# A hybrid decoder layer: the last gate chunk adds its earlier sums on VectorE instead of preloading them into PSUM, and two gate steps are held back around the last transposes

## The chip, the cores and the metric

The kernel runs on one core of one Trainium2 chip. The metric is the time of one execution on the device in microseconds (us), as the median of several runs. Besides, one execution was profiled: its trace gives the start and length of each engine's instructions, and its span, from the first to the last of them, is a little shorter than its time.

TensorE (PE in the profile; its weight loads are PEld) multiplies, VectorE (DVE) and ScalarE (ACT) work on elements, GpSimd (POOL) does too but cannot read PSUM, and SyncE (SP) issues the loads and the stores.

## The reference, cut to what matters

The layer has 256 tokens and a width of 2048, all in float32. The change lies in its last two formulas:

```
h    = h + HierMoE(RMSNorm(h))                 # 32 experts, each token goes to two
gate = sigmoid(RMSNorm(h, norm_ple) @ W_g)     # W_g: 2048 x 2048 (w_ple_gate)
out  = h + gate * (p @ W_p)                    # p @ W_p is ready long before
```

Each expert ends in a product with its `w_down` (512 x 2048). The sum over the experts is `h`, and the gate multiplies `h`, scaled by `norm_ple`, with `W_g`. The factor of the RMSNorm that belongs to a token is applied at the end, as the scale of the sigmoid, so that the product can begin before all of `h` is there.

## The kernel before

The kernel is written for one instruction order, engine by engine: what stands first in the code is issued first on its engine, and nothing reorders it. All weights flow through one ring of 26 buffers of 1 MB. `want` lists the loads in the order in which SP issues them, `pump` issues as many as have a buffer, and `free` gives buffers back.

The columns of `h` are made in four chunks of 512 (`TC`, numbers 0 to 3). Experts are handled in eight waves of four (`w` = 0 to 7). At the end of the program the columns of chunks 2 and 3 still miss the waves 4 to 7. `down_wave(w, ...)` (L1103) is the product of one wave with 512 columns of `w_down`: 32 matmuls at L1109 that need four loads of 1 MB. `outputs` (L1062) evicts it as a high part `yh` (ScalarE, L1065) and a low part `yl` (VectorE, L1066), and `scatter` (L1069) adds both to the sum over waves, `po`. After wave 7, `add_down` (L1115) adds `po` to `h` (called `acc`, in the trace `x`), `rows(ci)` (L1136) transposes the chunk on TensorE (L1145), scales it (VectorE, L1148) and splits it into a high part (ScalarE, L1151) and a low part (VectorE, L1152), both in `hs`. `squares` (L1154) sums the squares for the RMSNorm.

The gate's product for a chunk `ci` is cut into eight steps (`pg_steps`): the step `k = 2n + q` multiplies 256 of the chunk's 512 rows of `W_g` (the half `q`) with the block `n` of 512 output columns. `gate_step` (L1160) is 12 matmuls of 128 x 512 (L1170 to L1172) over two token halves `tt`: high times high, high times low, low times high. `prep_pg` (L1125) prepares the weights of a step with `split` (L344): ScalarE casts the high part (L346), and then VectorE subtracts to get the low part (L347), into one of three buffers `wsq`. It is called one and two steps ahead. Two steps complete a block: for chunks 0 to 2 VectorE then adds it to the sum so far, `gs` (L1196; `macc` in the trace).

These 24 steps of the chunks 0 to 2 stand in the list `todo`, and `steps(n)` takes the next `n` of them. They are strewn between the down waves as work for TensorE while loads and evictions go on. `W_g` arrives in loads of 1 MB, two for each half of a chunk's 2048 output columns; `halves_` says behind which down wave's loads each pair stands.

The last chunk comes when `todo` is empty. Its result must be the sum over all four chunks. `preload(n)` brings `gs` into the PSUM block by a product with the identity in float32 (L1275, two matmuls, four records in the trace), and the chunk's own steps add to it there. A finished block goes through the sigmoid (ScalarE, L1300, straight from PSUM), is multiplied by `ple` and added to `acc` (VectorE, L1301 and L1302), and is stored (SP, L1303).

Of the kernel before, what the change touches and what calls it, by code (L numbers as in the profile page):

```python
# [11 lines left out]
AF = mybir.ActivationFunctionType  # L12
# [18 lines left out]
def kernel(ctx: ExitStack, tc: tile.TileContext, I, out):  # L31
    nc = tc.nc
# [28 lines left out]
    loads, nxt, arrived = [], [0], {}  # L61
# [18 lines left out]
    def free(n=1):  # L80
        used[0] -= n
        pump()

    def ps():
        return PS.tile([128, 512], F32, name="pst", tag="ps")

    def pa():
        return PA.tile([128, 2, 512], F32, name="pat", tag="pa")

    def w2(shape, name, dt=F32):  # L90
        return W.tile(shape, dt, name=name, tag="w2", bufs=4)
# [79 lines left out]
                want(("ple", k), [128, 2048], w_ple[128 * k:128 * k + 128, :])  # L171

    order = [(2, w) for w in range(NROW, NW)] + [(3, w) for w in range(NROW, NW)]
    halves_ = [(0, 1), (1, 0), (1, 1), (2, 0), None, (2, 1), None, (3, 0)]
    for (ci, w), nxt_ in zip(order, halves_):
        want_d(w, *TC[ci])
        if nxt_:
# [39 lines left out]
    ident = C.tile([128, 128], F32, name="ident")  # L217
# [125 lines left out]
    def split(i, src, shape, eng=nc.vector, copy=nc.scalar.copy):  # L343
        wsl.append(wsl.pop(0))  # L344
        t = wsl[-1].rearrange("p (a s b) -> p a s b", a=shape[0], s=2)
        copy(t[:, :, 0], src)  # L346
        eng.tensor_sub(t[:, :, 1], src, t[:, :, 0].bitcast(F32))  # L347
        wsp[i] = t
# [448 lines left out]
    for i, (kind, a, b, q) in enumerate(granules):  # L797
        if i < n_in:
            group, start, stop = a, b == 0 and q == 0, b == 1 and q == 1
        else:  # L800
            group, start, stop = "o", (i - n_in) % 4 == 0, (i - n_in) % 4 == 3
# [5 lines left out]
        pt = pts[group]  # L807
# [292 lines left out]
    rs5 = C.tile([128, 2, 1], F32, name="rs5")  # L1100
    last = len(TC) - 1
# [13 lines left out]
    def add_down(po, c0, cn):  # L1115
        for tt in range(2):
            nc.vector.tensor_add(acc[tt][:, c0:c0 + cn], po[:, tt], acc[tt][:, c0:c0 + cn])

    def pg_steps(ci):
        return [(n, q) for n in range(4) for q in range(TC[ci][1] // 256)]  # L1120
# [4 lines left out]
    def prep_pg(ci, i):  # L1125

        upto = granules.index((ci, 0)) + i
        while done[0] <= min(upto, len(granules) - 1):
            c, k = granules[done[0]]
            done[0] += 1  # L1130
            n, q = pg_steps(c)[k]
            split((c, k), arrived["pg", c, n // 2, q][:, :, 512 * (n % 2):512 * (n % 2) + 512], [2, 512])
            if n % 2:
                free()

    def rows(ci):  # L1136

        c0, cn = TC[ci]
        kn, k0 = cn // 128, c0 // 128
        hs = hsb[ci % 2]  # L1140
        src = []
        for tt in range(2):
            src.append(ps().rearrange("p (k t) -> p k t", k=4))
            for kk in range(kn):
                nc.tensor.transpose(src[tt][:, kk], acc[tt][:, c0 + 128 * kk:c0 + 128 * kk + 128], ident)  # L1145
        for tt in range(2):
            tm = w2([128, 4, 128], "tm")
            nc.vector.tensor_tensor(tm, src[tt],  # L1148
                                    g_ple[:, k0:k0 + kn, None].to_broadcast([128, kn, 128]), op=OP.mult)
            hh = hs[:, :, 128 * tt:128 * tt + 128]  # L1150
            nc.scalar.copy(hh, tm)  # L1151
            nc.vector.tensor_sub(hs[:, :, 256 + 128 * tt:384 + 128 * tt], tm, hh.bitcast(F32))  # L1152

    def squares(ci):  # L1154
        c0, cn = TC[ci]
        for tt in range(2):
            scr = w2([128, 512], "scr")
            nc.scalar.activation(scr, acc[tt][:, c0:c0 + cn], AF.Square, accum_out=ss5[:, tt, ci:ci + 1])

    def gate_step(ci, i, pt, start):  # L1160
        n, q = pg_steps(ci)[i]
        kn = TC[ci][1] // 128
        hs = hsb[ci % 2]
        ws = wsp.pop((ci, i))
        for tt in range(2):
            for kk in range(2):
                b = 2 * q + kk
                mh = hs[:, b, 128 * tt:128 * tt + 128]
                ml = hs[:, b, 256 + 128 * tt:384 + 128 * tt]
                nc.tensor.matmul(pt[tt], mh, ws[:, kk, 0], start=start and b == 0, stop=False)  # L1170
                nc.tensor.matmul(pt[tt], mh, ws[:, kk, 1], start=False, stop=False)  # L1171
                nc.tensor.matmul(pt[tt], ml, ws[:, kk, 0], start=False, stop=b == kn - 1)  # L1172

    def two(kind):
        if kind:
            return [ps(), ps()]
        pt = pa()
        return [pt[:, 0], pt[:, 1]]

    def gate_product(ci):  # L1180
        kq = TC[ci][1] // 256
        steps = pg_steps(ci)
        for i, (n, q) in enumerate(steps):
            prep_pg(ci, i + 1)
            if q == 0:
                pt = two(n % 2)
            gate_step(ci, i, pt, True)
            if (ci, i + 2) < (last - 1, len(steps)):
                prep_pg(ci, i + 2)
            ns = slice(512 * n, 512 * n + 512)  # L1190
            if q == kq - 1:
                for tt in range(2):
                    if ci == 0:
                        nc.scalar.copy(gs[tt][:, ns], pt[tt])
                    else:
                        nc.vector.tensor_add(gs[tt][:, ns], pt[tt], gs[tt][:, ns])  # L1196
            yield
# [6 lines left out]
    for w in range(NW):  # L1204
# [10 lines left out]
        if w == NW - 2:  # L1215
            for n in range(4):
                for tt in range(2):
                    ns = slice(512 * n, 512 * n + 512)
                    nc.vector.tensor_add(hmid[tt][:, ns], macc[tt][:, ns], hmid[tt][:, ns])
            gs = macc  # L1220
# [10 lines left out]
    todo = [next_ for ci in range(last) for next_ in [gates[ci]] * len(pg_steps(ci))]  # L1231

    def steps(n):
        for _ in range(n):
            next(todo.pop(0))
# [17 lines left out]
    rows(2)  # L1253
    steps(1)
    squares(2)
    steps(3)
    po = pa()
    for w in range(NROW, NW):
        y = down_wave(w, *TC[3])
# [5 lines left out]
        scatter(po, w, y, w == NROW, w == NW - 1)  # L1265
        if w < NW - 1:
            steps(1)
    assert not todo
    early = [two(0), None, two(1), None]

    def preload(n):
        if early[n] is None:
            early[n] = two(n // 2)
        for tt in range(2):
            nc.tensor.matmul(early[n][tt], ident, gs[tt][:, 512 * n:512 * n + 512], start=True, stop=False)  # L1275

    ci = last
    preload(0)
    add_down(po, *TC[ci])
    rows(ci)  # L1280
    prep_pg(ci, 1)
    preload(1)
    preload(2)
    squares(ci)
    nc.vector.tensor_reduce(rs5, ss5[:, :, 0:4], axis=AX.X, op=OP.add)
    nc.scalar.activation(rs5, rs5, AF.Sqrt, bias=eps, scale=1.0 / D)
# [1 line left out]
    nc.vector.reciprocal(rs5, rs5)  # L1288
    so = [alloc([128, 4, 512], F32, "so") for _ in range(2)]
    for n in range(4):  # L1290
        if n == 3:
            preload(3)
        for q in range(2):
            prep_pg(ci, 2 * n + q + 1)
            gate_step(ci, 2 * n + q, early[n], False)
            prep_pg(ci, 2 * n + q + 2)
        ns = slice(512 * n, 512 * n + 512)
        for tt in range(2):
            sg = so[tt][:, n]
            nc.scalar.activation(sg, early[n][tt], AF.Sigmoid, scale=rs5[:, tt])  # L1300
            nc.vector.tensor_mul(sg, sg, ple[tt][:, ns])  # L1301
            nc.vector.tensor_add(sg, sg, acc[tt][:, ns])  # L1302
            nc.sync.dma_start(out[128 * tt:128 * tt + 128, ns], sg)  # L1303
# [132 lines left out]
```

## Time and profile before

| | |
|---|---|
| median of 3 runs | 1364.64 us (1362.74 to 1364.91) |
| the profiled execution, its own time | 1363.11 us |
| its span | 1361.3 us |
| mean granted TensorE clock | 0.926 of 2.4 GHz |
| PE busy | 1136.3 us (83%) |
| VectorE, ScalarE, GpSimd busy | 411.8, 266.3, 122.4 us |
| loads and stores | 484.29 MB, mean 356 GB/s |

The times in the rows count from the start of the span. A share of busy time is a mean over stages with different limits. What counts here is the last 130 us, and there which wait ends last. GpSimd computes nothing in these 130 us.

### The profile page before, as it was taken

What the parts mean: (1) busy time and instruction counts of PE and PEld (TensorE: products, weight loads), DVE (VectorE), ACT (ScalarE), POOL (GpSimd) and SP (SyncE); (2) the same over time, 40 slices, a digit from 0 to 9 for tenths busy, and PEclk for the clock granted to TensorE, in tenths of its full rate; (3) what the DMA queues carried; (4) which work ended last, traced back from release to release, by engine and by line L of the source; (5) the groups of instructions that cost most, each with busy time, mean ns of one, the idle gap of its engine ahead of it and who ended that gap; (6) DMA issues with size and microseconds to landing.
All of it is one profiled execution on the core that took longest, in us unless ns stands there. A gap on an engine that the chain in (4) does not pass through costs nothing.

```text
span 1361.3 us, 14898 instructions
## 1 busy us (share of the span) xinstructions
PE 1136.3 (83%) x6123; PEld 634.3 (47%) x6124; DVE 411.8 (30%) x623; ACT 266.3 (20%) x435; POOL 122.4 (9%) x150
## 2 busy tenths in 40 slices
PE   7999999999998786768678766875986876689997
PEld 6888777888663251215125221511531521126755
DVE  6746887655411210201111020110110120124636
ACT  5435555444101000000000000000020000024324
POOL 2214567000000000000000000000000000000000
PEclk9999999999998888789888878989989888889999
DMA  8992237876899999999999999999999999999981
GB/s 256 317 341 73 84 124 249 322 241 226 340 422 420 422 422 421 421 421 422 421 422 421 422 420 422 414 420 422 413 420 421 415 420 421 414 396 393 392 337 64
DMA packets 133141, 484.29 MB, mean 356 GB/s; under 512 B 12020, under 2 KB 49292, under 8 KB 92876
## 3 DMA queue, kind: packets, MB, share of 16 engines
q1 hardware_dynamic: 132204, 480.89, 89.5%
q0 software_dynamic: 864, 2.40, 0.5%
q8 instruction: 50, 0.82, 0.3%
q14 instruction: 23, 0.19, 0.0%
HBM read 478.80 MB, written 4.19 MB: 355 GB/s over the span
## 4 chain that ended last, share of the span: by engine, by line
DMA 49%; PE 39%; DVE 5%; ACT 3%; SPq 2%; issue 1%; POOL 1%; DVEq 0%; ACTq 0%
DMA ld<-in_w_up_dram 35%; DMA ld<-in_w_down_dram 13%; PE pat L770 6%; PE pst L949 5%; PE pat L965 4%; PE pat L771 3%; PE pst L1109 2%; PE pat L748 2%; PE pat L750 2%; PE pat L749 2%; SPq L76 1%; ACT wsp L346 1%; PE pst L1092 1%; PE pat L1170 1%; PE pat L1171 1%
## 5 line engine op out<-in xcount | busy, mean ns | idle before, releaser
L965 PE MATMUL pat<-ld,xg 128*32 128x512 f32 x2048 | 325.6, 669 | 104.4 <-DMA ld<-in_w_up_dram 55.3
L965 PEld LDWEIGHTS pat<-ld,xg 128*32 128x32 f32 x2048 | 77.2, 120 | 341.6 <-issue 152.5
L770 PE MATMUL pat<-xs,wsp 128*128 128x512 f32 x544 | 196.7, 404 | 0.0
L1025 PE MATMUL pst<-ld,wv 128*32 128x512 f32 x768 | 152.2, 755 | 52.1 <-DMA ld<-in_w_down_dram 47.1
L347 DVE TENSOR_TENSOR wsp<-ld,wsp 128x1024 fp32r<-128x1024 f32 x91 | 131.3, 1446 | 81.3 <-ACT wsp L346 77.9
L771 PE MATMUL pat<-xs,wsp 128*128 128x256 f32 x544 | 153.9, 283 | 0.4 <-DVE wsp L347 0.4
L951 DVE TENSOR_TENSOR xg<-pst,gffn 128x512 f32<-128x512 f32 (+1 forms) x33 | 22.3, 676 | 393.8 <-PE pst L949 393.8
L346 ACT CAST wsp<-ld 128x1024 fp32r<-128x1024 f32 x104 | 108.1, 1048 | 89.2 <-PE pat L750 44.0
L949 PEld LDWEIGHTS pst<-sel,x 128*128 128x128 f32 x512 | 112.7, 311 | 8.7 <-issue 5.4
L770 PEld LDWEIGHTS pat<-xs,wsp 128*128 128x128 f32 x544 | 103.5, 190 | 27.6 <-issue 2.8
L949 PE MATMUL pst<-sel,x 128*128 128x128 f32 x512 | 114.8, 384 | 0.0
L1025 PEld LDWEIGHTS pst<-ld,wv 128*32 128x32 f32 x768 | 34.5, 132 | 163.7 <-DMA ld<-in_w_down_dram 93.3
L1002 ACT ACTIVATE sg<-pat 128x512 f32<-128x512 f32 x8 | 4.8, 597 | 519.9 <-PE pat L965 519.8
L771 PEld LDWEIGHTS pat<-xs,wsp 128*128 128x128 f32 x544 | 104.0, 191 | 1.2 <-DVE wsp L347 1.2
L1066 DVE SCALAR_TENSOR_TENSOR yl<-pst,sw,yh 128x512 fp32r<-128x512 f32 x32 | 23.9, 746 | 232.8 <-ACT yh L1065 232.8
L1065 ACT ACTIVATE yh<-pst,sw 128x512 fp32r<-128x512 f32 x32 | 22.0, 688 | 242.6 <-PE pst L1025 184.7
L942 POOL TENSOR_TENSOR sel<-sel,et 128x128 f32<-128x128 f32 x16 | 6.1, 400 | 643.0 <-DVE sel L940 643.0
L1072 PE MATMUL pat<-yl,wv 128*128 128x512 f32 x64 | 31.8, 496 | 27.4 <-DVE yl L1066 27.4
L748 PE MATMUL pat<-wsp,mx 128*128 128x512 f32 (+1 forms) x128 | 49.8, 389 | 0.1
L750 PE MATMUL pat<-wsp,mx 128*128 128x512 f32 (+1 forms) x128 | 49.0, 383 | 0.0
L749 PE MATMUL pat<-wsp,mx 128*128 128x512 f32 (+1 forms) x128 | 49.0, 383 | 0.0
L347 DVE TENSOR_TENSOR wsq<-ld,wsq 128x1024 fp32r<-128x1024 f32 x32 | 38.6, 1222 | 16.0 <-ACT wsq L346 16.0
(271 smaller groups left out, 1069.5 us busy)
## 6 DMA issues: line engine op xcount, KB each, us to landing
ld<-in_w_gate_dram SPq DMA_DIRECT2D x128, 1024.0 KB, 19.8
ld<-in_w_up_dram SPq DMA_DIRECT2D x128, 1024.0 KB, 11.1
ld<-in_w_down_dram SPq DMA_DIRECT2D x128, 1024.0 KB, 19.8
ld<-in_w_in_dram SPq DMA_DIRECT2D x35, 1024.0 KB, 12.4
ld<-in_w_out_dram SPq DMA_DIRECT2D x16, 1024.0 KB, 8.1
ld<-in_w_ple_gate_dram SPq DMA_DIRECT2D x16, 1024.0 KB, 17.0
x<-in_x_dram SPq DMA_DIRECT2D x8, 256.0 KB, 6.6
spill<-x POOLq DMA_DIRECT2D x8, 256.0 KB, 5.4
```

The source lines that it names most:

```text
L346: copy(t[:, :, 0], src)
L347: eng.tensor_sub(t[:, :, 1], src, t[:, :, 0].bitcast(F32))
L748: nc.tensor.matmul(o, mh, ws[:, kk, 0, cs], start=first, stop=False)
L749: nc.tensor.matmul(o, mh, ws[:, kk, 1, cs], start=False, stop=False)
L750: nc.tensor.matmul(o, ml, ws[:, kk, 0, cs], start=False, stop=last)
L770: nc.tensor.matmul(pt[:, b, :], ws[:, kk, 0, bs], xk, start=first, stop=False)
L771: nc.tensor.matmul(pt[:, b, 0:256], ws[:, kk, 1, bs], xk[:, 0:256], start=False, stop=last)
L949: nc.tensor.matmul(pt[:, 128 * jj:128 * jj + 128], hmid[tt][:, j::16], sel[w][:, tt], start=tt == 0, stop=tt == 1)
L965: nc.tensor.matmul(pt[32 * e:32 * e + 32, n, :], g[:, j, 32 * e:32 * e + 32], wt, start=j == 0, stop=j == 15, tile_position=(0, 32 * e))
L1025: nc.tensor.matmul(pts[n][32 * e:32 * e + 32, :], hv[:, j, 32 * e:32 * e + 32], d[:, 512 * n:512 * n + 512], start=j == 0, stop=j == 3, ti ...
L1072: nc.tensor.matmul(po[:, tt], sT(w)[:, 128 * tt:128 * tt + 128], y[i], start=start and i == 0, stop=stop and i == 1)
L1109: nc.tensor.matmul(pt[32 * e:32 * e + 32, :], hv[:, j, 32 * e:32 * e + 32], arrived["d", 4 * w + e, c0][:, j, :], start=j == 0, stop=j == ...
```

## The change

It has four parts:

- The pair of loads of the second half of chunk 2's `W_g` stands behind the loads of wave 6 of chunk 3 instead of wave 5.
- Two gate steps fewer are taken before the down waves of chunk 3 (`steps(1)` for `steps(3)`). All later steps stand two places further back in the work, and the two that are left over are taken after the last wave: one behind `add_down`, one behind `rows`.
- In the last chunk the low part of the odd steps (`k % 2`) is subtracted by GpSimd, not by VectorE. `last` is 3.
- The preloads are gone. A block of the last chunk starts from zero; VectorE adds `gs` to it on its way out of PSUM into `sg`, and the sigmoid reads `sg`. The block's PSUM is taken when it starts.

```diff
-    halves_ = [(0, 1), (1, 0), (1, 1), (2, 0), None, (2, 1), None, (3, 0)]
+    halves_ = [(0, 1), (1, 0), (1, 1), (2, 0), None, None, (2, 1), (3, 0)]
...
             n, q = pg_steps(c)[k]
-            split((c, k), arrived["pg", c, n // 2, q][:, :, 512 * (n % 2):512 * (n % 2) + 512], [2, 512])
+            split((c, k), arrived["pg", c, n // 2, q][:, :, 512 * (n % 2):512 * (n % 2) + 512], [2, 512],
+                  nc.gpsimd if c == last and k % 2 else nc.vector)
...
     squares(2)
-    steps(3)
+    steps(1)
     po = pa()
...
+    ci = last
+    add_down(po, *TC[ci])
+    steps(1)
+    rows(ci)
+    steps(1)
     assert not todo
-    early = [two(0), None, two(1), None]
-
-    def preload(n):
-        if early[n] is None:
-            early[n] = two(n // 2)
-        for tt in range(2):
-            nc.tensor.matmul(early[n][tt], ident, gs[tt][:, 512 * n:512 * n + 512], start=True, stop=False)
-
-    ci = last
-    preload(0)
-    add_down(po, *TC[ci])
-    rows(ci)
     prep_pg(ci, 1)
-    preload(1)
-    preload(2)
     squares(ci)
...
     for n in range(4):
-        if n == 3:
-            preload(3)
+        pt = two(n % 2)
         for q in range(2):
             prep_pg(ci, 2 * n + q + 1)
-            gate_step(ci, 2 * n + q, early[n], False)
+            gate_step(ci, 2 * n + q, pt, True)
             prep_pg(ci, 2 * n + q + 2)
...
-            nc.scalar.activation(sg, early[n][tt], AF.Sigmoid, scale=rs5[:, tt])
+            nc.vector.tensor_add(sg, pt[tt], gs[tt][:, ns])
+            nc.scalar.activation(sg, sg, AF.Sigmoid, scale=rs5[:, tt])
             nc.vector.tensor_mul(sg, sg, ple[tt][:, ns])
             nc.vector.tensor_add(sg, sg, acc[tt][:, ns])
```

On SP the last 28 loads of the program stand like this before (`w_down` in `ld` is a load for a down wave, `w_ple_gate` one of `W_g`; a wave's four loads are one x4):

```order
L76 DMA ld<-in_w_down_dram 128x4x512 x4
L76 DMA ld<-in_w_ple_gate_dram 128x2x1024 x2
L76 DMA ld<-in_w_down_dram 128x4x512 x8
L76 DMA ld<-in_w_ple_gate_dram 128x2x1024 x2
L76 DMA ld<-in_w_down_dram 128x4x512 x8
L76 DMA ld<-in_w_ple_gate_dram 128x2x1024 x4
```

and like this now:

```order
L76 DMA ld<-in_w_down_dram 128x4x512 x4
L76 DMA ld<-in_w_ple_gate_dram 128x2x1024 x2
L76 DMA ld<-in_w_down_dram 128x4x512 x12
L76 DMA ld<-in_w_ple_gate_dram 128x2x1024 x2
L76 DMA ld<-in_w_down_dram 128x4x512 x4
L76 DMA ld<-in_w_ple_gate_dram 128x2x1024 x4
```

The loads of wave 6 of chunk 3 have moved two places forward; those of wave 7, the last x4 of `w_down` (split off the x8), stand where they stood, with four loads behind them.

On VectorE, between the low part of wave 7's output (`yl`) and the scaling of the first transposed rows (`tm`), before (`wsq_...` is a step's weights, its number the buffer; `x_75` and `x_76` are the two token halves of `acc`):

```order
L1066 SCALAR_TENSOR_TENSOR yl<-pst,sw,yh 128x512
L347 TENSOR_TENSOR wsq_5891<-ld,wsq_5891 128x2x512
L1196 TENSOR_TENSOR macc<-pst,macc 128x512 x2
L1117 TENSOR_TENSOR x_75<-pat,x_75 128x512
L1117 TENSOR_TENSOR x_76<-pat,x_76 128x512
L1148 TENSOR_TENSOR tm<-pst,vT 128x512
```

and now (L1197 is the former L1196, L1149 the former L1148):

```order
L1066 SCALAR_TENSOR_TENSOR yl<-pst,sw,yh 128x512
L347 TENSOR_TENSOR wsq_5893<-ld,wsq_5893 128x2x512
L1197 TENSOR_TENSOR macc<-pat,macc 128x512 x2
L347 TENSOR_TENSOR wsq_5891<-ld,wsq_5891 128x2x512
L1117 TENSOR_TENSOR x_75<-pat,x_75 128x512
L1117 TENSOR_TENSOR x_76<-pat,x_76 128x512
L1149 TENSOR_TENSOR tm<-pst,vT 128x512
```

One more weight split, that of the last held-back step, stands ahead of `add_down` (L1117).

On VectorE in the last chunk, a middle block before (two splits and then the two token halves of `so`, which is `sg`):

```order
L347 TENSOR_TENSOR wsq_5892<-ld,wsq_5892 128x2x512
L347 TENSOR_TENSOR wsq_5893<-ld,wsq_5893 128x2x512
L1301 TENSOR_TENSOR so<-so,ple 128x512
L1302 TENSOR_TENSOR so<-so,x_75 128x512
L1301 TENSOR_TENSOR so<-so,ple 128x512
L1302 TENSOR_TENSOR so<-so,x_76 128x512
```

and now (L1292 is the new addition, L1294 and L1295 are the former L1301 and L1302):

```order
L347 TENSOR_TENSOR wsq_5892<-ld,wsq_5892 128x2x512
L1292 TENSOR_TENSOR so<-pst,macc 128x512
L1294 TENSOR_TENSOR so<-so,ple 128x512
L1295 TENSOR_TENSOR so<-so,x_75 128x512
L1292 TENSOR_TENSOR so<-pst,macc 128x512
L1294 TENSOR_TENSOR so<-so,ple 128x512
L1295 TENSOR_TENSOR so<-so,x_76 128x512
```

One of the two splits has gone to GpSimd. ScalarE's sigmoid of a token half now lies between that half's L1292 and L1294, and the second half's L1292 stands behind the first half's L1295.

## Rows read from the trace of the kernel before

**Rows 1.** The page's head: span and number of instructions.
```profile
span 1361.3 us, 14898 instructions
```
**Rows 2.** Three stretches: busy time by engine, then TensorE's granted clock, DMA share, GB/s.
```profile
1280.00:1300.00 20.00, 20.00 (x120) 11.97 (x119) 9.66 (x12) 5.36 (x6) 0.00 (x0) 1.00 1.04 392
1300.00:1320.00 20.00, 20.00 (x115) 12.03 (x114) 6.39 (x9) 3.67 (x5) 0.00 (x0) 1.00 1.02 387
1320.00:1340.00 20.00, 19.23 (x77) 13.18 (x76) 13.79 (x20) 12.47 (x19) 0.00 (x0) 1.00 0.17 68
```
**Rows 3.** The chain that ended last, waves 5, 6, 7 of chunk 3: start, us, what.
```profile
1293.91 3.57 PE pst L1109 x32
...
1304.10 4.06 PE pst L1109 x32
...
1314.78 4.18 PE pst L1109 x32
```
**Rows 4.** SP in order of time: last load of wave 5, and of wave 7.
```profile
1274.19 2.60 SPq L76 DMA_DIRECT2D ld<-in_w_down_dram  x1
...
1300.89 2.53 SPq L76 DMA_DIRECT2D ld<-in_w_down_dram  x1
```
**Rows 5.** The tile ld, 1250 to 1340 us: from a load's issue to its landing.
```profile
DMA to landing us min/median/max: 14.0/14.3/14.3
```
**Rows 6.** SP's waits from 1180 us: us in total, times, longest.
```profile
SPq L76 <- PE pst L1172: 9.8, 3, 4.3
```
**Rows 7.** The chain that ended last, from wave 7's evictions to the end.
```profile
1322.16 0.74 DVE wsq L347
...
1325.24 0.67 PE pst L1145 x4
...
1326.56 1.72 PE pat L1275 x4
...
1329.99 0.23 PE pat L1170
...
1346.73 1.72 PE pst L1275 x4
...
1355.42 0.69 DVE so L1302
```
**Rows 8.** Groups by line, 1253 us to the end: busy us, mean ns | idle before.
```profile
L347 DVE TENSOR_TENSOR wsq<-ld,wsq 128x1024 fp32r<-128x1024 f32 x22 | 26.5, 1221 | 7.2 <-ACT wsq L346 7.2
...
L1302 DVE TENSOR_TENSOR so<-so,x 128x512 f32<-128x512 f32 x8 | 5.5, 692 | 0.3
...
L1196 DVE TENSOR_TENSOR macc<-pst,macc 128x512 f32<-128x512 f32 x8 | 5.1, 682 | 0.0
...
L1158 ACT ACTIVATE scr<-x 128x512 f32<-128x512 f32 x4 | 2.5, 623 | 0.0
```
**Rows 9.** VectorE in order of time: first two splits inside the last chunk.
```profile
1334.45 2.36 DVE L347 TENSOR_TENSOR wsq<-ld,wsq 128x1024 fp32r<-128x1024 f32 x2 [2.29 <-ACT wsq L346]
```
**Rows 10.** GpSimd in order of time, two splits early in the program.
```profile
134.44 2.41 POOL L347 TENSOR_TENSOR wsp<-ld,wsp 128x1024 fp32r<-128x1024 f32 x1 [1.84 <-ACT wsp L346]
...
154.51 2.36 POOL L347 TENSOR_TENSOR wsp<-ld,wsp 128x1024 fp32r<-128x1024 f32 x1 [4.94 <-ACT wsp L346]
```
**Rows 11.** VectorE in order of time, beside those two.
```profile
135.39 2.54 DVE L347 TENSOR_TENSOR wsp<-ld,wsp 128x1024 fp32r<-128x1024 f32 x1 [1.36 <-ACT wsp L346]
...
154.95 0.69 DVE L395 TENSOR_TENSOR hS<-pat,lo 128x512 f32<-128x512 f32 x1 [2.17 <-ACT lo L394]
```
**Rows 12.** Stretches in which TensorE waited for loads, columns as in rows 2.
```profile
1083.00:1096.00 13.00, 7.49 (x54) 1.98 (x46) 1.38 (x2) 1.18 (x2) 0.00 (x0) 1.00 1.03 414
...
1202.10:1208.80 6.70, 5.80 (x25) 1.34 (x26) 0.75 (x1) 0.69 (x1) 0.00 (x0) 0.50 1.05 390
```
**Rows 13.** TensorE in order of time: one such wait.
```profile
1200.43 1.05 PE L1025 MATMUL pst<-ld,wv 128*32 128x512 f32 x2 [1.52 <-DMA ld<-in_w_down_dram]
```
**Rows 14.** Line 1025's matmuls, 1185 to 1209 us: duration ns min/median/max.
```profile
L1025 PE MATMUL pst<-ld,wv x48: 592/1061/1062, 1185.2 to 1208.9; 128*32 128x512 f32 x48
```

## The prediction

> **What bounds the kernel now.** I read the stretches of 20 us first, to see which engine is full in the part that the change touches. Up to 1320 us TensorE is busy all the time at full clock, and at the same time the DMA engines are full, at 387 to 392 GB/s; behind 1320 us the loads are over and TensorE goes on alone [rows 2]. So two things may bind up to 1320 us, and the chain of waits tells them apart: wave 5 of chunk 3 took 3.57 us, waves 6 and 7 took 4.06 and 4.18 us for the same 32 records [rows 3]. The 0.5 and 0.6 us more are waits for a load. SP issued wave 7's last load at 1300.89 us [rows 4], and a load lands 14.3 us after its issue [rows 5], that is at 1315.2 us, 0.4 us after TensorE had come to the wave (1314.78). TensorE and the loads are level there. Wave 5's last load was issued at 1274.19 [rows 4] and there at 1288.5, 5.4 us ahead of its use.
>
> From wave 7 the chain goes through VectorE to the last transposes (1325.24), through two preloads of 1.72 us to the first gate step of the last chunk (1329.99), then along TensorE with one more preload to the last block, and ends with L1302 at 1355.42 + 0.69 = 1356.1 [rows 7]. The span ends at 1361.3 [rows 1], so 5.2 us are the last store and the end of the program. The execution's own time, 1363.11, is 1.8 more than its span. I make the sum against 1363.11; the runs' median is 1.5 above it, and I add half of that at the end, since the profiled one is among the quicker.
>
> **Two steps held back, and the loads' order.** A gate step is 12 matmuls of 0.23 us [rows 7], 2.7 us. TensorE comes 5.5 us earlier to the waves of chunk 3. Wave 5: 1293.91 - 5.5 = 1288.4, level with its load (1288.5). Wave 6, 10.2 us later as before [rows 3]: 1298.7; its loads stand two places further forward, each place about 2.6 us [rows 4], so they are there at 1304.6 - 5.2 = 1299.4. The swap thus does its work, and costs nothing by itself: the delayed pair of W_g is there before wave 7's loads, and a cast that waits for it is covered by TensorE's next wait. Wave 7: ready at 1299.4 + 10.2 = 1309.6, but its last load keeps its place in the queue, behind the same bytes on a full DMA: 1315.2. So wave 7 ends as before, near 1318.9, and nothing is won ahead of it; TensorE has 5.6 us of idle time there instead of two steps, which now stand behind it. Bounds: if the load followed TensorE, up to 5.5 us won; none lost.
>
> **The clock.** What does this idle time cost? The clock was at half (1.2 GHz) from 1202 to 1209 us [rows 12], after waits of some 1.5 us for loads [rows 13]; at half clock a record of such a column-tiled matmul takes 1.06 us and at full clock 0.59 [rows 14], about 1.8 times. But from 1083 to 1096 us TensorE was idle for over 5 of 13 us and kept its full clock [rows 12]. Wave 7's 3.57 us would take up to 7.1 at half clock: a loss between 0 and 3.5 us. The idle time ahead of wave 7 is longer than the waits of 1202, so I take half of the upper end, 1.7 us. The Trainium skill (TensorE: Matmul & The Clock Gate, section "Why this matters for your kernels") asks for no long idle gaps between bursts of matmuls, since the clock then falls back. By that rule alone the loss is sure, and the time is 1.7 to 3.5 us above what it is with none; by the row of 1083 us it is none. [...]
>
> **Between wave 7 and the last chunk.** TensorE loses preloads 0, 1 and 2 here (5.2 us) and gains two steps (5.5 us). VectorE decides: one more split, 1.22 us [rows 8], stands ahead of add_down, so the transposes go from 1325.2 to 1326.4, and with 1.3 us of transposes and the second held-back step (2.7 us) the last chunk's first step starts at 1330.4 instead of 1330.0. The chain behind it on ScalarE and VectorE (squares, factor, casts) moves by the same 1.2 us: the first split on VectorE inside the chunk, that of step 2, ended at 1334.45 + 1.22 = 1335.7 [rows 8, 9], now at 1336.9. Step 1 waits some 0.4 us for GpSimd's split (2.4 us [rows 10] for 1.22 on VectorE), which ends no later than this.
>
> **The last chunk: VectorE in series.** Before, ScalarE took a block straight from PSUM and VectorE had four operations and two splits for each. Now each token half is a chain on VectorE that holds up everything behind it, since VectorE works in order: addition of gs 0.64 to 0.68 (L1196 is the same operation [rows 8]), sigmoid on ScalarE 0.62 (as L1158, also from SBUF [rows 8]), two operations of 0.69 (as L1302 [rows 8]), and three handovers of about 0.04 us. That is 2.75 us, in which VectorE idles for the sigmoid: the second half's addition stands behind the first half's end. A block is 5.5 us, and with its one split 6.7, where TensorE's two steps are 5.46. VectorE becomes the bound; the casts behind the sigmoids on ScalarE and the splits come late too, so TensorE waits for it, and the removed preload 3 (1.72 us) wins nothing. From 1336.9: eight halves of 2.75 are 22.0, two more splits 2.4; the end is at 1361.3, against 1356.1: 5.2 us later.
>
> **GpSimd beside VectorE.** Early in the program VectorE's split took 2.54 us beside GpSimd's: it ended at 137.93, 1.08 us after GpSimd's end at 136.85 [rows 10, 11]. So it made next to no progress during it. L395, with one operand in PSUM, took its usual 0.69 us within GpSimd's 2.36 [rows 10, 11]. Of the new chain the addition of gs is of the second kind; L1301 and L1302 read two tiles of SBUF like the split, and I cost them so. The Trainium skill (SBUF — State Buffer, section "Who interferes with whom") states this division: with two SBUF inputs VectorE contends with a GpSimd instruction that reads SBUF, with one it does not. No row shows L1301 beside GpSimd. GpSimd's splits of steps 3, 5 and 7 start with their casts, about when a block's first addition starts, and run 2.4 us; the first L1301 is due 1.3 us after that addition. It is held 0.7 to 1.0 us, less the 0.14 by which the held split was quicker at its end: 2.3 us for the three. Bounds: 0 (if L1301 runs like L395) and 3.
>
> **Sum.** 1363.1 + 5.2 (series) + 2.3 (GpSimd) + 1.7 (clock) = 1372.3, and 0.7 for the median's place: 1373.
>
> **The rivals.**
> - *TensorE sets the end.* If VectorE kept up with a block in under 5.46 us, TensorE would run from 1318.9 through two steps, scatter (four matmuls, 0.9), transposes (1.3), and nine steps in all behind these: 1318.9 + 5.5 + 0.9 + 1.3 + 2.7 + 21.8 = 1351.1, and a last half of 2.75 and 0.3 us of handover: 1354.2, 1.9 us before today's 1356.1. That gives 1361.2, 1362 with the median's place: not slower. For it: VectorE is busy 14 of 20 us in this stretch [rows 2], so by busy time there is room. Against it: its order, in which the sigmoid's time is idle. Its point is 5.46 us for a block; I find 6.7. Chance 0.05.
> - *The loads follow TensorE.* SP waited 9.8 us in three goes for TensorE to free buffers [rows 6]; if these waits and not the DMA engines set the landing, wave 7 starts up to 5.5 us earlier and idles less: 1373 - 5.5 - 1.7 = 1366. Against it: 387 to 392 GB/s without a break [rows 2] and the constant 14.3 us. Chance 0.05.
> - *The clock holds*: 1371. Chance 0.15.
> - *GpSimd does not hold up VectorE*: 1370.7. Chance 0.1.
> - *The clock falls again in the last chunk*, where TensorE now waits 1 to 2 us in each block, and wave 7 is slow as a whole: 1.8 more for wave 7 and up to 3 for a slow pair of steps (5.5 us more, less 2.5 us that it waited anyway): 1375 to 1378. Chance 0.15.
>
> That the change does something else than it says is excluded by the orders shown.
>
> **How the numbers follow.** The forecast as summed has 0.5. A change of 0.2% (2.7 us) is about what a measurement of this kernel can tell. Slower by more than that are all cases but the first two rivals: 0.9, and a little of the second, 0.91. The first lies at the edge: faster 0.03, same 0.02; the second is same: 0.04. The range from 1368 to 1378 takes in all bounds of the series with either of its two additions, and leaves out the first two rivals and the upper end of the last.
>
> **What would show it.** Right: wave 7 starts at the old time with TensorE idle 5 us ahead of it; L1295's last end is 7 us or more later after wave 7 than before; VectorE's idle time ahead of L1294 is attributed to ScalarE; TensorE waits for L347 and L346 in steps 4 and 6; L1294 beside GpSimd lasts over 1 us; the clock row around 1315 us is at half. Wrong: wave 7 before 1312 us, TensorE without waits in the last chunk, or blocks that follow each other on VectorE in 5.5 us.

## The result, and the profile after

The changed kernel takes 1372.64 us (median of 4 runs, 1372.39 to 1375.29), the kernel before 1363.85 in the same comparison: a ratio of 1.0072, with an interval from 1.006 to 1.0084. It is slower by 0.72%, 8.8 us. The forecast was 1373.0 us.

The profiled execution of after has a span of 1370.9 us, 9.6 more than [rows 1]. I read it in the order of the prediction's steps. First three stretches (busy time by engine, then granted clock, DMA share and GB/s, as in [rows 2]):

```profile
1300.00:1320.00 20.00, 16.69 (x88) 7.97 (x81) 5.44 (x6) 3.84 (x4) 0.00 (x0) 0.91 1.02 390
1320.00:1340.00 20.00, 18.73 (x81) 13.88 (x80) 11.54 (x17) 11.89 (x18) 3.98 (x2) 1.00 0.14 55
1340.00:1370.90 30.90, 16.23 (x67) 12.00 (x65) 19.72 (x25) 8.83 (x11) 6.67 (x3) 0.87 0.19 70
```

Up to 1320 us TensorE, which was full before, now idles for 3.3 us beside an equally full DMA, at a lower mean clock. In the last stretch TensorE works up to 1359.2 us, with 2.9 us of waits, and VectorE goes on for another 6.4 us. TensorE's wave 7 of chunk 3 and its eviction on ScalarE, in order of time, are the first place:

```profile
1309.90 1.36 PE L1109 MATMUL pst<-ld,wv 128*32 128x512 f32 x4
1312.91 1.04 PE L1109 MATMUL pst<-ld,wv 128*32 128x512 f32 x2 [1.66 <-DMA ld<-in_w_down_dram]
1315.61 5.16 PE L1109 MATMUL pst<-ld,wv 128*32 128x512 f32 x26 [1.66 <-DMA ld<-in_w_down_dram]
...
1320.81 0.69 ACT L1065 ACTIVATE yh<-pst,sw 128x512 fp32r<-128x512 f32 x1 [13.43 <-PE pst L1109]
```

TensorE is there at 1309.9 (forecast 1309.6), and its last record to wait starts at 1315.6: the loads kept their time [rows 4]. Before the change the last wait, on PEld, and the eviction stood like this:

```profile
1315.33 2.28 PEld L1109 LDWEIGHTS pst<-ld,wv 128*32 128x32 f32 x25 [0.47 <-DMA ld<-in_w_down_dram]
...
1318.99 0.69 ACT L1065 ACTIVATE yh<-pst,sw 128x512 fp32r<-128x512 f32 x1 [9.17 <-PE pst L1109]
```

The eviction comes 1.8 us later. The end of the last wait accounts for 0.3 us (1315.61 for 1315.33), and the clock for the other 1.5 (stretches, columns as above):

```profile
1206.10:1315.33 109.23, 105.13 (x572) 64.35 (x564) 50.84 (x60) 38.88 (x56) 0.00 (x0) 1.00 1.04 392
1315.33:1318.74 3.41, 3.13 (x16) 0.79 (x20) 0.00 (x0) 0.00 (x0) 0.00 (x0) 0.50 1.02 407
1318.74:1363.10 44.36, 36.22 (x158) 26.22 (x150) 29.62 (x40) 20.00 (x28) 10.65 (x4) 1.00 0.18 70
```

Towards the end of the second of two waits of 1.66 us it goes to half (1.2 GHz), for 3.4 us, and is then at full speed up to the last matmuls. The 26 records behind the last wait take 5.16 us; in e_order below, after the same two waits but with the clock at 1.00, they take 3.62:

```profile
1315.10 3.62 PE L1109 MATMUL pst<-ld,wv 128*32 128x512 f32 x26 [1.66 <-DMA ld<-in_w_down_dram]
```

VectorE between wave 7 and the transposes, now:

```profile
1323.99 1.23 DVE L347 TENSOR_TENSOR wsq<-ld,wsq 128x1024 fp32r<-128x1024 f32 x1 [1.70 <-ACT wsq L346]
1325.13 1.28 DVE L1197 TENSOR_TENSOR macc<-pat,macc 128x512 f32<-128x512 f32 x2
1326.33 1.22 DVE L347 TENSOR_TENSOR wsq<-ld,wsq 128x1024 fp32r<-128x1024 f32 x1
1327.46 1.28 DVE L1117 TENSOR_TENSOR x<-pat,x 128x512 f32<-128x512 f32 x2
```

The second L347 is the split that did not stand there; `add_down` (L1117) starts at 1327.46, where before it started at 1324.50:

```profile
1324.50 1.28 DVE L1117 TENSOR_TENSOR x<-pat,x 128x512 f32<-128x512 f32 x2
```

Of these 3.0 us wave 7 brings 1.8 and the split 1.2. The last chunk on VectorE, its first block, and the last instruction:

```profile
1337.41 1.23 DVE L347 TENSOR_TENSOR wsq<-ld,wsq 128x1024 fp32r<-128x1024 f32 x1 [2.29 <-ACT wsq L346]
1338.56 0.68 DVE L1292 TENSOR_TENSOR so<-pat,macc 128x512 f32<-128x512 f32 x1
1340.03 1.42 DVE L1294 TENSOR_TENSOR so<-so,ple 128x512 f32<-128x512 f32 x1 [0.79 <-ACT so L1293]
1341.49 0.69 DVE L1295 TENSOR_TENSOR so<-so,x 128x512 f32<-128x512 f32 x1
1342.10 0.69 DVE L1292 TENSOR_TENSOR so<-pat,macc 128x512 f32<-128x512 f32 x1
1343.57 0.69 DVE L1294 TENSOR_TENSOR so<-so,ple 128x512 f32<-128x512 f32 x1 [0.79 <-ACT so L1293]
1344.30 0.69 DVE L1295 TENSOR_TENSOR so<-so,x 128x512 f32<-128x512 f32 x1
1344.91 1.22 DVE L347 TENSOR_TENSOR wsq<-ld,wsq 128x1024 fp32r<-128x1024 f32 x1
1346.05 0.68 DVE L1292 TENSOR_TENSOR so<-pst,macc 128x512 f32<-128x512 f32 x1
...
1364.87 0.69 DVE L1295 TENSOR_TENSOR so<-so,x 128x512 f32<-128x512 f32 x1
```

The series stands here as forecast: VectorE is idle for 0.79 us ahead of each L1294, for ScalarE's sigmoid (L1293), and the second half begins when the first has ended. In the 27.0 us from the first L1292 to the end of the last L1295 these eight waits are 6.3 us. From L1292 to L1292 a first half takes 3.54 us (1338.56 to 1342.10). One that GpSimd does not touch takes 2.80 (1359.87 to 1362.67, the last two). The difference is L1294: 1.42 in place of 0.69 us, in three blocks. GpSimd's four splits beside it:

```profile
1333.25 2.40 POOL L347 TENSOR_TENSOR wsq<-ld,wsq 128x1024 fp32r<-128x1024 f32 x1 [329.11 <-ACT wsq L346]
1338.42 2.49 POOL L347 TENSOR_TENSOR wsq<-ld,wsq 128x1024 fp32r<-128x1024 f32 x1 [2.77 <-ACT wsq L346]
1345.50 2.88 POOL L347 TENSOR_TENSOR wsq<-ld,wsq 128x1024 fp32r<-128x1024 f32 x1 [4.60 <-ACT wsq L346]
1352.98 2.88 POOL L347 TENSOR_TENSOR wsq<-ld,wsq 128x1024 fp32r<-128x1024 f32 x1 [4.60 <-ACT wsq L346]
```

The split of 1338.42 ends at 1340.91, and the L1294 that began at 1340.03 ends 0.54 us behind that. L1292, which reads PSUM, runs in its usual 0.68 us within the same split. And it works in both directions: the GpSimd split of 1345.50 starts while VectorE's own (1344.91 + 1.22) is under way, and lasts 2.88 instead of 2.40. That does not reach TensorE. TensorE waits for VectorE's own split, which has come late, in the first step of the third block (step 4), and by 1.15 us in that of the fourth:

```profile
1346.18 0.50 PE L1172 MATMUL pat<-wsq,hs 128*128 128x512 f32 x1 [1.16 <-DVE wsq L347]
```

From wave 7's eviction to the end of the last addition it is 44.75 us now (1320.81 to 1365.56), and was 37.1 (1318.99 to 1356.11). I use this length below, since it leaves out wave 7, the clock there and the last load: that wait ends at 1314.93 us in one of the profiled executions (e_pre) and at 1317.66 in another (e_vec).

### The profile page after: what moved, and what is told of

It reads as the page before. It is cut to its first block, busy times and chain, and to the rows that moved or that the text cites. A ratio compares the mean times of both kernels' runs of the same rounds, so it can differ in the third digit from the quotient of the medians.

```text
span 1370.9 us, 14886 instructions
## 1 busy us (share of the span) xinstructions
PE 1135.6 (83%) x6107; PEld 629.6 (46%) x6108; DVE 415.2 (30%) x627; ACT 266.5 (19%) x435; POOL 132.4 (10%) x154
## 4 chain that ended last, share of the span: by engine, by line
DMA 38%; PE 27%; issue 25%; DVE 6%; ACT 3%; POOL 1%; SPq 0%; POOLq 0%; DVEq 0%; ACTq 0%
DMA ld<-in_w_up_dram 26%; DMA ld<-in_w_down_dram 11%; PE pat L770 6%; PE pst L949 4%; PE pat L965 3%; PE pat L771 3%; PE pat L748 2%; PE pat L750 2%; PE pat L749 2%; ACT wsp L346 1%; DVE wsp L347 1%; ACT S L497 1%; PE pst L1025 1%; DVE S L478 1%; DVE so L1294 1%
## 5 line engine op out<-in xcount | busy, mean ns | idle before, releaser
L347 DVE TENSOR_TENSOR wsp<-ld,wsp 128x1024 fp32r<-128x1024 f32 x91 | 132.2, 1456 | 79.4 <-ACT wsp L346 79.4
L347 POOL TENSOR_TENSOR wsq<-ld,wsq 128x1024 fp32r<-128x1024 f32 x4 | 10.6, 2662 | 341.1 <-ACT wsq L346 341.1
```

## The experiments

All are versions of the changed kernel, unless said. "1370.49 (1.0055; 1.0042 to 1.0068)" is a median and its ratio to the kernel before, with its interval.

**The series: both additions first (e_order).**

```diff
         for tt in range(2):
             sg = so[tt][:, n]
             nc.vector.tensor_add(sg, pt[tt], gs[tt][:, ns])
             nc.scalar.activation(sg, sg, AF.Sigmoid, scale=rs5[:, tt])
+        for tt in range(2):
+            sg = so[tt][:, n]
             nc.vector.tensor_mul(sg, sg, ple[tt][:, ns])
```

Expected: 

> The changed kernel, with the last blocks' operations in another order: for each block both additions of gs with their sigmoids first, then both multiplications and last additions. Theory (VectorE in series with the sigmoid sets the pace): a block is 2 x 0.68 for the additions, 0.12 of waiting until the first sigmoid is done (0.68 + 0.72 + 0.08 after the first addition's start, 1.48), 4 x 0.69, one split of 1.23, and 0.73 where GpSimd holds an operation: 6.2 us in place of 7.48 for three blocks, 4.2 for the last one. From the first addition at 1338.56 that is 3 x 6.2 + 4.2 = 22.8 us where it was 27.0: 1368.5. Rival (TensorE's waits come from the splits, and the order on VectorE doesn't matter, since it is busy for the same time): 1372.6. Second rival (it becomes TensorE's pace of 5.46 us a block, with the hold covered): 1366.5.

Measured: 1367.82 (1.0044; 1.0032 to 1.0057), 40.4 us from wave 7's eviction to the last addition's end (1318.76 to 1359.11) where it was 44.75. VectorE, and GpSimd's split of the same moment:

```profile
1338.00 1.42 DVE L1296 TENSOR_TENSOR so<-so,ple 128x512 f32<-128x512 f32 x1 [0.20 <-ACT so L1293]
...
1340.78 2.82 DVE L1297 TENSOR_TENSOR so<-so,x 128x512 f32<-128x512 f32 x1
```

```profile
1340.67 2.38 POOL L347 TENSOR_TENSOR wsq<-ld,wsq 128x1024 fp32r<-128x1024 f32 x1 [1.80 <-ACT wsq L346]
```

The idle time in a block falls from 2 x 0.79 to 0.20 us, and the gain, 4.4 us, is close to the theory's 4.1. The next GpSimd split now starts 0.1 us ahead of an L1297, which is held for 2.1 us. So the order of the same operations is worth half of the loss.

**GpSimd's hold: one operand in PSUM (e_psum).**

```diff
-            nc.scalar.activation(sg, sg, AF.Sigmoid, scale=rs5[:, tt])
-            nc.vector.tensor_mul(sg, sg, ple[tt][:, ns])
+            nc.scalar.activation(pt[tt], sg, AF.Sigmoid, scale=rs5[:, tt])
+            nc.vector.tensor_mul(sg, pt[tt], ple[tt][:, ns])
```

Expected: 

> The changed kernel, with the sigmoid written back into the PSUM tile, so that the multiplication reads one operand from PSUM and one from SBUF. Same operations, same order. Theory (GpSimd's split holds a VectorE operation with two SBUF inputs, and not one with an operand in PSUM): the three multiplications of 1.42 us go to 0.69, the last addition behind each is held by less than 0.1 because GpSimd's split is then over: 2.2 us less, 1370.4. Rival 1 (GpSimd slows any VectorE operation beside it): the three stay at 1.42, 1372.6. Rival 2 (what is held is whatever two-input SBUF operation comes next, for as long as the split lasts): the hold goes to the last addition in full, 1372.6 too, but with L1295 at 1.4 and L1294 at 0.69.

Measured: 1370.49 (1.0055; 1.0042 to 1.0068). The first block's multiplication and addition:

```profile
1340.71 0.69 DVE L1294 TENSOR_TENSOR so<-pat,ple 128x512 f32<-128x512 f32 x1 [0.76 <-ACT pat L1293]
1341.43 0.72 DVE L1295 TENSOR_TENSOR so<-so,x 128x512 f32<-128x512 f32 x1
```

GpSimd's split ran from 1339.12 to 1341.61. Within it the multiplication that reads PSUM takes 0.69 us; the addition, with two operands in SBUF, lies within its last 0.18 us and takes 0.72. From eviction to end it is 42.4 us (1321.52 to 1363.93), 2.3 less: the theory's 2.2. The Trainium skill (SBUF — State Buffer, section "Who interferes with whom") says that a VectorE instruction with two SBUF inputs contends with a GpSimd one that reads SBUF and that one with at most one does not; this pair of runs, 1.42 against 0.69 us for the same multiplication, agrees.

**No GpSimd (e_vec).**

```diff
-            split((c, k), arrived["pg", c, n // 2, q][:, :, 512 * (n % 2):512 * (n % 2) + 512], [2, 512],
-                  nc.gpsimd if c == last and k % 2 else nc.vector)
+            split((c, k), arrived["pg", c, n // 2, q][:, :, 512 * (n % 2):512 * (n % 2) + 512], [2, 512])
```

Expected: 

> The changed kernel with all subtractions of the last chunk on VectorE, none on GpSimd. Theory (a hold of 0.73 us in three blocks): nothing lasts 1.42 us any more, a block has a second split of 1.23: 2 x 2.80 + 2 x 1.23 = 8.06 us for three blocks in place of 7.48, so 1.7 us more: 1374.3. Rival 1 (the 1.42 us is not GpSimd's doing): it stays, and three splits of 1.23 come on top: 1376.3. Rival 2 (TensorE's waits for GpSimd's splits of 2.4 to 2.9 us set the pace): without them the last chunk is shorter, 1370 to 1372.

Measured: 1374.97 (1.0093; 1.0078 to 1.0108), 46.7 us from eviction to end (1321.32 to 1368.03). VectorE's two splits ahead of the first block, and the multiplication that was held:

```profile
1338.66 2.36 DVE L347 TENSOR_TENSOR wsq<-ld,wsq 128x1024 fp32r<-128x1024 f32 x2 [2.29 <-ACT wsq L346]
...
1342.42 0.69 DVE L1293 TENSOR_TENSOR so<-so,ple 128x512 f32<-128x512 f32 x1 [0.79 <-ACT so L1292]
```

The 1.42 is gone, and VectorE has the splits of the odd steps again: 2.0 us more against 1.7 expected. So GpSimd is worth having even with its hold: what a split takes off VectorE (1.2 us) is more than the 0.73 that it costs there.

**The clock: matmuls in the waits (e_warm, then e_warm2).** In `down_wave`, for wave 7 of chunk 3 alone, with a PSUM tile `wm` that nobody reads:

```diff
         for j in range(4):
             for e in range(4):
+                if wm is not None and j == 0:
+                    for _ in range((5, 5, 4, 0)[e]):
+                        nc.tensor.matmul(wm, hsb[0][:, 0, 0:128], hsb[0][:, 1], start=True, stop=True)
```

e_warm has 5 ahead of all four. Expected of it: 

> The changed kernel with 20 matmuls of 128 x 128 by 512 (0.23 us each, into a PSUM tile that nobody reads) in the waits of wave 7 of chunk 3, five ahead of each of its first four records. Theory (the idle time ahead of wave 7 halves the clock, and that is 1.8 us): the granted clock stays at 1.00 around 1315 to 1319, wave 7's eviction comes at 1319.0 in place of 1320.8, and the rest follows: 1370.8. Rival (the eviction is late because loads land later, not because of the clock): clock up, eviction still at 1320.8, 1372.6 or, by the time of the added matmuls, up to 1 more.

Measured: 1373.78 (1.008; 1.0067 to 1.0093), no gain: the clock stayed at 1.00, but the last five matmuls stood ahead of the records of the fourth load until 1316.96, while the last load, issued at 1300.24, was there at 1314.5 by the 14.3 us of [rows 5]. So the clock was held at the price of wave 7, and the run tells nothing apart. Without these five:

Expected: 

> The changed kernel with 14 matmuls of 0.23 us that nobody reads in the waits of wave 7 of chunk 3: 5, 5 and 4 ahead of its first three records, none ahead of the fourth, so that they end before the last load lands. Theory (the clock is what makes wave 7 late): granted clock 1.00 around 1315 to 1319 in the profiled execution, wave 7's eviction about 3.9 us after its last wait's end where it was 5.2, 1371 as the median where executions with a held clock are in it already, 0.5 to 1.8 less than the changed kernel. Rival (the loads' landing sets it, the clock is a detail): no difference, 1372.6.

Measured: 1370.98 (1.0053; 1.0039 to 1.0067). TensorE, and a stretch with its clock:

```profile
1315.15 3.82 PE L1113 MATMUL pst<-ld,wv 128*32 128x512 f32 x28
```

```profile
1316.00:1319.00 3.00, 3.00 (x25) 1.24 (x17) 0.00 (x0) 0.00 (x0) 0.00 (x0) 1.00 1.01 404
```

28 records take 3.82 us where 26 took 5.16, and the eviction starts at 1319.01, as before the change (1318.99). From there to the end it is 44.73 us (to 1363.74), as in the changed kernel (44.75): only wave 7 has changed.

**The held-back steps alone undone (e_nohold).**

```diff
-    halves_ = [(0, 1), (1, 0), (1, 1), (2, 0), None, None, (2, 1), (3, 0)]
+    halves_ = [(0, 1), (1, 0), (1, 1), (2, 0), None, (2, 1), None, (3, 0)]
...
     squares(2)
-    steps(1)
+    steps(3)
...
     add_down(po, *TC[ci])
-    steps(1)
     rows(ci)
-    steps(1)
```

Expected: 

> The changed kernel with the held-back part alone undone: three steps ahead of chunk 3's waves and the loads' old order, as before the change; still no preloads, sums on VectorE, odd splits on GpSimd. Theory (holding back costs 1.8 us by the clock and 1.2 us by one more split ahead of the transposes, and hides nothing that the last chunk needs): no idle time ahead of wave 7, full clock, transposes at 1325.2, the first split in the chain on VectorE ends near 1335.7 and not 1338.6, and the rest is the same: 1369.7. Rival (TensorE must have these steps between wave 7 and the last chunk, or its waits there grow by as much): 1372.6.

Measured: 1371.16 (1.0052; 1.0038 to 1.0066). From eviction to end it is 43.9 us (1320.17 to 1364.02), 0.9 less, not 1.2. The steps' absence opens a gap elsewhere; TensorE, and the stretch behind the gap:

```profile
1326.43 0.90 PE L1146 MATMUL pst<-ident,x 128*128 128x128 f32 x4 [2.41 <-DVE x L1117]
```

```profile
1326.00:1333.00 7.00, 6.02 (x18) 4.54 (x19) 3.75 (x7) 3.42 (x7) 1.29 (x1) 0.55 0.00 0
```

With neither a preload nor a held-back step TensorE idles for 2.41 us ahead of the transposes, its clock falls there (1.00 in the changed kernel), and the transposes take longer; in the second profiled execution of this kernel, below, it is the same (2.39 us, 0.57 from 1326 to 1333). This points to the step behind `add_down`: it filled this gap. With 0.9 us saved for 1.2, it was worth some 0.3 us; the split ahead of `add_down` costs 1.2.

Since such differences lie within the intervals, three kernels were timed once more, on one chip.

Expected of the changed kernel: 

> The changed kernel once more, on the same chip as the two that follow, since what they differ by is less than the intervals of runs on several chips: 1372.0 to 1373.0, 0.65 to 0.75% slower than before.

Of e_warm2: 

> The kernel of e_warm2 once more, beside the changed kernel. Theory (the fallen clock costs up to 1.8 us in the executions in which it falls): 1 to 1.8 us less than the changed kernel. Rival (what was seen was the chip or the place of the loads): no difference.

Of e_nohold: 

> The kernel of e_nohold once more, beside the changed kernel. Theory (holding back costs the clock's 1.7 us, and 0.9 us by the split ahead of the transposes, as the profiles show): 1.5 to 2.6 us less than the changed kernel. Rival (its idle time ahead of the transposes takes most of it back): less than 1 us.

Measured: 1373.27 (1.0073; 1.0059 to 1.0086), 1370.90 (1.0057; 1.0044 to 1.0071) and 1370.43 (1.0058; 1.0044 to 1.0072). The first and the two others differ by some 0.15% of the ratio, 2.1 us (by the medians 2.4 and 2.8). The intervals overlap, so this comparison does not show the difference by itself; the earlier one had the same sign (1.0072 against 1.0053 and 1.0052), and the profiles give each a cause. Its size is not known to better than 1 or 2 us. By the ratio, e_nohold lies in the theory's range and e_warm2 a little above its 1 to 1.8 us. The first again has the clock at half after its two waits (0.56 from 1316 to 1319 us).

**The held-back steps alone made (e_pre).** The kernel of before, with the two edits of e_nohold's diff in the other direction, and preloads in this order:

```diff
     ci = last
     preload(0)
     add_down(po, *TC[ci])
+    steps(1)
     rows(ci)
+    steps(1)
+    assert not todo
     prep_pg(ci, 1)
     preload(1)
     preload(2)
```

Expected: 

> The kernel of before with the held-back part alone: two steps held back around the last transposes and the loads' new order; preloads into PSUM as before (the first ahead of the transposes, the second and third behind the second step), all splits on VectorE. Theory: with the preloads kept, TensorE is the bound behind wave 7: from 1320.8 it has a step (2.73), scatter (0.93), a preload (1.72), a step, transposes (1.31), and behind them what before had there: the first step of the last chunk at 1336.4 in place of 1330.0, so 1363.1 + 6.4 + 0.7 = 1370.2 (1.8 less where the clock holds). Rival (it is the missing preloads that cost, and held-back steps alone cost only 3.0 us, clock and split): 1366.8.

Measured: 1371.63 (1.0058; 1.0044 to 1.0072). TensorE's preloads behind wave 7:

```profile
1327.07 3.41 PE L1274 MATMUL pat<-macc,ident 128*128 128x512 f32 x4 [1.80 <-DVE macc L1196]
...
1338.64 1.88 PE L1274 MATMUL pst<-macc,ident 128*128 128x512 f32 x4
```

The third preload ends at 1340.5, where the last chunk's first step stood at 1329.99 [rows 7]. Half clock, a wait of 1.8 us for VectorE, and a preload mostly at half speed (3.41 us) add to what I had summed. So holding back on its own costs nearly as much as the whole change. The two parts do not add up: from eviction to end it is 44.84 us here (1321.41 to 1366.25), 43.9 without the held-back steps and 44.75 with both; by the ratios both together cost some 2 us more than either alone (1.0072 against 1.0058 and 1.0052), with intervals that overlap. In the changed kernel VectorE sets the pace of the last chunk, and TensorE has room for the held-back steps.

**What the runs point to, together (e_early_psum).** e_nohold with the order of e_order and the sigmoid into PSUM of e_psum, and at the last wave:

```diff
         if w == NW - 1:
             nc.scalar.activation(junk, eps, AF.Sqrt)
-        steps(1)
-        if w == NW - 1:
             prep_pg(last, 0)
+        else:
+            steps(1)
         scatter(po, w, y, w == NROW, w == NW - 1)
...
     add_down(po, *TC[ci])
     rows(ci)
+    steps(1)
```

Expected: 

> What the runs so far point to, together: the changed kernel without the held-back steps, with both additions of a block ahead of its multiplications, the sigmoid written back into PSUM, and chunk 3's last scatter, add_down and transposes brought ahead of the one step that stands behind wave 7. Theory (the chain behind wave 7 on VectorE sets the time, TensorE has room): wave 7 ends at 1318.9, yl 1.5 later, scatter 0.9, add_down 1.4, transposes end near 1324, 2.5 us earlier than before, first step of the last chunk at 1327.8 in place of 1330.0; a block is 4.2 + 1.23 = 5.5 us on VectorE, level with TensorE's 5.46; eight steps (21.8) to 1349.7, then 3.2 us of tail: last addition at 1353 in place of 1356.1: 1360 to 1362. Rival (VectorE with GpSimd's splits beside it cannot keep this pace, blocks of 6.2): 2.2 us more, 1363 to 1364, no gain over the kernel before.

Measured: 1368.39 (1.0032; 1.002 to 1.0044): a miss by 7 us of the theory, and by some 5 of the rival. VectorE, then TensorE:

```profile
1337.70 0.69 DVE L1291 TENSOR_TENSOR so<-pat,macc 128x512 f32<-128x512 f32 x1 [0.76 <-ACT pat L1292]
...
1341.20 2.82 DVE L1296 TENSOR_TENSOR so<-so,x 128x512 f32<-128x512 f32 x1
```

```profile
1345.22 0.50 PE L1172 MATMUL pat<-wsq,hs 128*128 128x512 f32 x1 [3.35 <-DVE wsq L347]
```

Two of my edits work against each other: in a block whose halves share one PSUM tile (`pat`), the second half's addition now waits for the first half's sigmoid, which writes into that tile. And GpSimd again starts 0.1 us ahead of an addition with two SBUF operands and holds it for 2.1 us; the split behind it is late, and TensorE waits 3.35 us. The clock falls here too: TensorE waits 2.57 us ahead of the transposes, and the granted clock is 0.50 from 1322.9 to 1329.3 us. No run tells apart how much of the miss is which. As long as GpSimd and VectorE share the last chunk, small shifts decide who holds whom.

**One preload less, where it is on the path (e_blk2).** The kernel of before; the third block is summed by VectorE, and the fourth is preloaded in its place:

```diff
-    early = [two(0), None, two(1), None]
+    early = [two(0), None, None, two(1)]
...
     preload(1)
-    preload(2)
+    preload(3)
...
-        if n == 3:
-            preload(3)
+        if n == 2:
+            early[2] = two(0)
...
+            if n == 2:
+                nc.vector.tensor_add(sg, early[n][tt], gs[tt][:, ns])
```

(The third block's step starts from zero, its sigmoid reads `sg`, and all blocks have the order of e_order.) Expected: 

> The kernel of before with one preload less, and only where it stood on TensorE's path: the fourth block's preload takes the place of the third's, ahead of the last chunk, where VectorE is still at work on the step's operands; the third block's sums are added by VectorE as in the change, both halves first, with no split left to do behind them. Nothing is held back, all splits stay on VectorE. Theory (TensorE sets the pace of the last chunk before the change, and its only preload there costs 1.72 us; VectorE was idle for 3.62 us ahead of the last block): 1.7 us less than the kernel before, 0.13%: 1362.0 where that gives 1363.7. Rival (the added sums delay the last block on VectorE or the splits ahead of it): no change, or 1 us more.

Measured: 1361.41 against 1362.64 (0.9986; 0.9977 to 0.9995): a little faster than the kernel before, by 0.14% where 0.13% was expected (1.9 us by the ratio, 1.2 by the two medians). VectorE in its third and fourth block:

```profile
1347.94 1.28 DVE L1301 TENSOR_TENSOR so<-pat,macc 128x512 f32<-128x512 f32 x2
1349.42 0.69 DVE L1305 TENSOR_TENSOR so<-so,ple 128x512 f32<-128x512 f32 x1 [0.19 <-ACT so L1302]
...
1352.53 0.69 DVE L1305 TENSOR_TENSOR so<-so,ple 128x512 f32<-128x512 f32 x1 [0.36 <-ACT so L1302]
```

and in the fourth block before:

```profile
1353.34 0.69 DVE L1301 TENSOR_TENSOR so<-so,ple 128x512 f32<-128x512 f32 x1 [3.62 <-ACT so L1300]
```

The additions fill time that VectorE had: it waits 0.36 us ahead of the last block where it waited 3.62. From eviction to the last addition's end it is 35.3 us (1320.00 to 1355.30) for 37.1, 1.8 less.

## Why the prediction was right, point by point

- **Wave 7's loads** keep their time: right (last issue 1301.02 us, 1300.89 before [rows 4]). The idle time ahead of the last record was over-sized: 3.3 us and not 5.6, since I had forgotten that the wave's first six records run in it; the sign of 5 us of idle time did not come true.
- **The clock**: it fell as forecast, 1.7 us for 1.5 in the profiled execution, but the size is luck. I took half of the upper end because the idle time would be longer than the waits of 1.5 us around 1202; it came as two waits of 1.66 us, hardly longer. The other stretch of [rows 12] was no better guide: its idle time comes in waits of at most 2.34 us. And it is no fixed price. Of the six profiled executions with these waits and nothing in them (the changed kernel twice, e_psum, e_pre, e_order, e_vec) four show half clock at wave 7 and two show 1.00, with waits of the same 1.66 us. The 26 records take 5.16, 5.03, 6.41 and 6.45 us in the four and 3.62 in the two: a price of 1.4 to 2.8 us or none, 1.4 in the mean. So the rival in which the clock holds is real too, for a third of them. The medians with filled waits, some 2 us lower, are in line with this.
- **One more split ahead of `add_down`**: right, 1.2 us. That a held-back step also fills a gap was not in the prediction: without these steps TensorE's clock falls ahead of the transposes (e_nohold).
- **VectorE in series**: right. A half takes 2.80 us (2.75 forecast; the sigmoid from SBUF takes 0.72 us, not the 0.62 that I took from L1158, which is another function and has no scale for each token). e_order shows that it is the order: with the same operations it gives 4.4 us back.
- **GpSimd holds VectorE**: right, 3 x 0.73 = 2.2 us for 2.3; e_psum takes it away with one operand's place.
- **The sum**: the last addition ends 9.45 us later (1365.56 for 1356.11), the sum said 9.2. In parts: 1.5 clock, 0.3 the end of the last load's wait (not in the sum), 1.2 split, 2.2 GpSimd, and the rest, 4.3, for the longer chain in the last chunk (4.0 in the sum, its 5.2 less the split).
- **The rivals**: TensorE does not set the end (its last matmul ends at 1359.2 us, 6.4 ahead of the last addition's end, and it waits for VectorE in steps 4 and 6 as forecast); the loads do not follow TensorE (it comes to wave 7 4.8 us earlier, and the last load is issued 0.13 us later); the clock does not fall again in the last chunk, although TensorE waits 1.16 us in a step there (1.00 up to 1363.1 us).

What stays open is why the clock falls in some executions and not in others after the same waits, and how much of the spread between runs (1370.93 to 1373.74 in the second set) is clock and how much the landing of the last load.

## What to carry to other kernels

When work moves from one engine to another that runs in order, sum the receiving engine's chain in issue order, with the time in which it waits for a third engine, and not its busy time: here a VectorE that is idle for 6.3 of 27.0 us was the bound. Of several like pieces only those on the path are worth moving: one of four preloads was, and moving one block's sum into VectorE's idle time won 0.14%, where moving all four lost 0.5 to 0.6% (e_nohold), and the whole change 0.72%. And a step that is taken away ahead of a transfer wins nothing if the transfer has its own pace; the idle time can even cost, through the clock.

## What the runs showed of the hardware that was not expected

- In the changed kernel the clock went to half for 3.4 us, late in the second of two waits of 1.66 us, 2.7 us apart; in e_psum and e_pre it was at half for some 6.8 us, also from within the second wait on, and in e_order and e_vec it stayed at 1.00. With 14 short matmuls in the waits it stayed at 1.00 in both executions of e_warm2. It also fell around a single wait of 2.4 us, in both executions of e_nohold. The Trainium skill (TensorE: Matmul & The Clock Gate, section "Why this matters for your kernels") asks for no long idle gaps between bursts; the trace agrees that gaps cost the clock, and shows it fall at gaps of 1.66 us, though not each time.
- The hold between GpSimd and VectorE goes both ways, and lasts for nearly all of the other's instruction: GpSimd's split took 3.48 us in e_order when VectorE's split of 1.22 us had started at the same time (1348.79), and VectorE's addition 2.82 us when it came 0.1 us behind GpSimd's.
- A float32 preload takes 3.41 us where the clock is mostly at half (e_pre, 1327.07 us; 0.59 from 1326.8 to 1330.5), and 1.88 in the same run at 1338.64 us.
